# Seven products of a pair in another order: the summed weight block first, three products in one bank

## The chip, the cores and the metric

The kernel runs on one core of one Trainium2 chip. The metric is the device time of one execution in microseconds (us); the figure of a kernel is the median of its runs. Five engines have their own instruction queues: TensorE (PE, with PEld for its weight loads), VectorE (DVE), ScalarE (ACT), GpSimd (POOL) and SyncE (SP). SP, POOL and ACT also start DMA transfers.

## The reference, cut to what matters

One layer of a streaming encoder with 512 frames and a model width of 2048, all in float32:

```
proj = rmsnorm(x) @ w_in          # split into q, k, v, gates, index parts
a = sparse_attention(...) * silu(az)
b = retention(...)        * silu(rz)
merged = sigmoid(ga) * (a @ w_a_out) + sigmoid(gb) * (b @ w_b_out)
r = x + merged @ w_o
y = r + (p @ w_ple) * sigmoid(r @ w_ple_gate)     # then a last rmsnorm
```

The change concerns five of these products: the columns rz, gb, ga and half of az of `w_in`, and `w_o`. Each is a product of a weight of 2048 rows with 512 moving columns.

## The kernel before, in words

**Precision.** A float32 operand is split into a rounded part and the rest (`h`, `l` of a weight, by ACT on line 138 and DVE or POOL on line 144), and the products are summed in PSUM.

**A pair.** The five products above are done two output blocks of 128 at a time, by a scheme of the Strassen-Winograd kind: instead of eight products of quarter size a pair takes seven. The weights of a pair are four blocks of 1024 rows by 128 columns, B11, B12, B21 and B22. The function `block_pair` says how seven stationary operands (units) come out of four raw buffers: buffer `w11` holds B11 and later B11+B12, buffer `t` holds B12+B22, then B11 more, then B21 more, and `w21`, `w22` hold their blocks. Only sums are made on this side. A sum with a block is made by a DMA from HBM that accumulates into the buffer (`add_block`, line 106, issued on POOL's queue: 512 KB each, three for a pair, one of them right after the buffer's first load); the sum of `t` and `w21` is made by DVE (line 146).

**Units ahead.** `gemm_pair` calls `split_to(i + AHEAD)` and `load_to(i + AHEAD + LOADS)` with AHEAD 4 and LOADS 5. So while unit i is multiplied, unit i+3 is split and the raw buffers of unit i+8 are asked for. There are four `wh` and `wl` tiles (W_BUFS), hence the split of a unit waits until the product four units before it is done, and seven raw buffers (RAW_BUFS). The rest of a split (the `wl` subtraction, then the sum into the raw buffer) is queued one step later.

**The moving side.** `combos` makes seven moving operands out of quarters of the input (`PRODUCTS` names them), each 512 wide: 256 columns rounded and 256 columns of rest. For the 22 pairs of `w_in` the input is the normalized x; its operands are made long before, kept in HBM and loaded again during the last retention head (tiles `ha`, `hs`, line 832). For the 8 pairs of `w_o` the input is `merged`; its operands (`ma`, `ms`) are made in four steps for each k, and the last of eight k is made while the first product of the first pair runs.

**A product** is eight k, each one matmul of 512 columns with `wh` (line 253) and one of 256 columns with `wl` (line 254). I count the seven products of a pair as product 0 to product 6. They go into four PSUM banks p, v, q, r in the order p, v, q, r, p, v, r. Behind each product stands what `after` lists: ACT copies (`e1` of p after product 0, `pv` of v after 1, `e2` of p after 4, line 223), DVE combinations (`e_t`, line 227, after products 2, 4, 5 and 6, and `e_d`, line 232, after product 3: r minus pv, which frees r for product 6). `done` adds the two halves of a combination into the output: one DVE addition for the gate pairs (line 854), two for `w_o` (lines 1074 and 1075).

**Order of work.** The order on each queue is the order in which the program writes its instructions; no planner moves them. Every k of a product calls `step`, which runs small pieces of other stages from the lists `todo`, `soon` and `bg`.

Of the kernel before, what the change touches and what calls it, by code (L numbers as in the profile page):

```python
# [9 lines left out]
F32 = mybir.dt.float32  # L10
# [3 lines left out]
AF = mybir.ActivationFunctionType  # L14
OP = mybir.AluOpType
# [19 lines left out]
def block_kernel(tc, xT, pT, posb, posq, w_in, w_v, w_ik, w_a, w_b, w_o, w_ple, w_gate,  # L35
                 w_gt, w_pt, fgb, tab, gains, cst, dec, out, out_a, out_b):
    nc = tc.nc
    pe, dve, act, pool, sp = nc.tensor, nc.vector, nc.scalar, nc.gpsimd, nc.sync

    with contextlib.ExitStack() as ctx:  # L40
# [10 lines left out]
        def U(name, dt=F32):  # L51
            return up.tile([128, L], dt, name=name, tag="u")

        def B(name, dt=F32):
            return bp.tile([128, 1280], dt, name=name, tag="b")

        def P(name):
            return pp.tile([128, L], F32, name=name, tag="p")
# [17 lines left out]
        def raw(src, k0, nk, cols, plus=None):  # L76
            raws.append((src, k0, nk, cols, plus))
            return len(raws) - 1
# [9 lines left out]
        def block_pair(s1, s2):  # L88

            b11, b12, b21, b22 = (s1, 0), (s2, 0), (s1, 8), (s2, 8)
            first = len(units)
            w11 = raw(*b11, 8, 128)
            t = raw(*b12, 8, 128, b22)
            w21, w22 = raw(*b21, 8, 128), raw(*b22, 8, 128)
            for r, plus in ((w11, b12), (t, b11), (w21, None), (w11, None), (t, w21), (t, None), (w22, None)):
                units.append((r, plus, 8, 128))
            return list(range(first, first + 7))

# [22 lines left out]
        def split_to(n):  # L123
            while state["split"] < min(n, len(units)):
                i = state["split"]
                load_to(i + 1)
                r, plus, nk, cols = units[i]
                if r in unfinished:
                    unfinished[r]()
                raw = view(raw_tiles[r], nk, cols)  # L130
                if i in in_raws:
                    t = wp.tile([128, 2, 512], F32R, name="whl", tag="wraw", bufs=RAW_BUFS)
                    h, l = t[:, 0:1], t[:, 1:2]
                elif nk * cols == L:
                    h, l = (U(n, F32R).rearrange("p (a c) -> p a c", c=cols) for n in ("wh4", "wl4"))
                else:
                    h, l = (view(wp.tile([128, 8, 128], F32R, name=n, tag=n), nk, cols) for n in ("wh", "wl"))
                act.activation(h, raw, AF.Copy)  # L138
                e = pool if nk * cols == 1024 and any(a <= i < b for a, b in pool_units) else dve

                def rest(r=r, plus=plus, e=e, l=l, raw=raw, h=h):
                    if unfinished.pop(r, None) is None:
                        return
                    e.tensor_sub(l, raw, h.bitcast(F32))  # L144
                    if isinstance(plus, int):
                        dve.tensor_add(raw, raw, view(raw_tiles[plus], nk, cols))
                    elif plus is not None:
                        add_block(r, plus)

                unfinished[r] = rest  # L150
                later(1 if e is dve else 2, rest)
                loaded[i] = (h, l)
                state["split"] += 1
# [7 lines left out]
        def later(n, f):  # L161
            if n <= 0:
                return f()
            tick[1] += 1
            heapq.heappush(soon, (tick[0] + n, tick[1], f))

        def step():
            tick[0] += 1
            while soon and soon[0][0] <= tick[0]:
                heapq.heappop(soon)[2]()  # L170
            f = todo.popleft() if todo else None
            if f is not None:
                f()
            elif bg and tick[0] % state["rate"] == 0:
                bg.popleft()()
# [34 lines left out]


        LO, HI = slice(0, 256), slice(256, 512)
        PRODUCTS = ("a11", "s3", "a12", "s1", "s2", "a22", "s4")

        def gemm_pair(ids, X, done):


            p, v, q, r = (P("ps_" + n) for n in ("p", "v", "q", "r"))
            E = {}

            def copy(n, src):
                E[n] = U(n)
                act.activation(E[n], src, AF.Copy)

            def out(f, x, y, i, c):
                t = U("e_t")
                f(t, x, y)
                done(t[:, LO], t[:, HI], i, c)

            def fourth():  # L230
                E["d"] = U("e_d")
                dve.tensor_sub(E["d"], r, E["pv"])  # L232

            def fifth():
                copy("e2", p)
                out(dve.tensor_sub, E["d"], E["e2"], 1, HI)

            after = {
                0: lambda: copy("e1", p),
                1: lambda: copy("pv", v),  # L240
                2: lambda: out(dve.tensor_add, q, E["e1"], 0, LO),
                3: fourth,
                4: fifth,
                5: lambda: out(dve.tensor_add, v, E["e2"], 0, HI),
                6: lambda: out(dve.tensor_sub, r, E["e2"], 1, LO),
            }
            for n, (i, o) in enumerate(zip(ids, (p, v, q, r, p, v, r))):
                split_to(i + AHEAD)
                load_to(i + AHEAD + LOADS)
                h, l = loaded[i]  # L250
                for k in range(8):
                    x = X[PRODUCTS[n]][k]
                    pe.matmul(o, h[:, k], x, start=(n < 4 and k == 0), stop=False, skip_group_check=True)  # L253
                    pe.matmul(o[:, LO], l[:, k], x[:, LO], start=False, stop=(k == 7), skip_group_check=True)  # L254
                    step()
                if n in after:
                    after[n]()

        def combos(lo, hi, name, keep=None):


            X = {n: [None] * 8 for n in PRODUCTS}
            T = {}

            def parts(n, k, src):
                t = U(name + n, F32R)
                act.activation(t[:, LO], src, AF.Copy)
                dve.tensor_sub(t[:, HI], src, t[:, LO].bitcast(F32))
                if keep is None:
                    X[n][k] = t  # L270
                else:
                    later(2, lambda: sp.dma_start(keep(n, k), t.bitcast(F32)))

            def sums(k):
                x, y = lo(k), hi(k)
                t1, t2 = T[k] = U("t1"), U("t2")
                dve.tensor_sub(t2[:, LO], x[:, LO], x[:, HI])
                dve.tensor_sub(t1[:, LO], x[:, HI], y[:, HI])
                dve.tensor_sub(t1[:, HI], t1[:, LO], x[:, LO])
                dve.tensor_add(t2[:, HI], y[:, LO], t1[:, HI])  # L280

            def one(k, i):
                if i == 0:
                    parts("a11", k, lo(k)[:, LO])
                    parts("a12", k, hi(k)[:, LO])
                elif i == 1:
                    sums(k)
                    parts("s3", k, T[k][1][:, LO])
                elif i == 2:
                    parts("s1", k, T[k][0][:, LO])  # L290
                    parts("s2", k, T[k][0][:, HI])
                else:
                    parts("s4", k, T.pop(k)[1][:, HI])
                    parts("a22", k, hi(k)[:, HI])

            return X, one
# [10 lines left out]
        for h in range(NH):  # L307
# [4 lines left out]
            else:  # L312
                ids = [block(col(g, h)[:, k:k + 8, :], (8,)) for k in (0, 8) for g in (RQ, RK)]
# [28 lines left out]
        for k in range(KT):  # L342
            if k in (1, 2, 4, 8, 12):
                load_to(state["raw"] + 1)
            if k < 10:
                t = U("xk")
                sp.dma_start(t, xT[:, k, :])
                xs.append(t)
            elif k % 2 == 0:
                t = B("xk2")  # L350
# [287 lines left out]
        hd = dp.tile([56, 128, L], F32, name="hd")  # L638
        x_at = {(n, k): hd[8 * i + k] for i, n in enumerate(PRODUCTS) for k in range(8)}
        xn = {}  # L640
# [183 lines left out]

        Xh = {n: [None] * 8 for n in PRODUCTS}
        x_wanted = collections.deque((n, k) for n in PRODUCTS for k in range(8))

# [36 lines left out]
        for n, u in enumerate(u_rz):  # L864
            y = B("y2")
# [177 lines left out]
        for m in PAIRED:  # L1043
            t = B("sm")
            s, o = t[:, 0:512], t[:, 512:1024]
# [17 lines left out]
        for m in range(8):  # L1063
# [9 lines left out]
            def done(c0, c1, i, q, xc=xc):  # L1073
                dve.tensor_add(xc[i][:, q], xc[i][:, q], c0)
                dve.tensor_add(xc[i][:, q], xc[i][:, q], c1)

            if m == 7:
                todo.extend([None] * 24)
                for k in range(2):
                    t = U("pk")  # L1080
# [9 lines left out]
        for m in range(MF):  # L1090
            i = u_p[m // 4][0]
# [5 lines left out]
            for k in range(2):  # L1097
                a, b = pparts[k]
# [5 lines left out]
            t = U("pw")  # L1104
# [84 lines left out]
        for j in range(4):  # L1189
            pw = P("ps_pw")  # L1190
            wide(u_t[1], pparts, [pw], [j], False)
            y = ys[MF + j]
# [3 lines left out]
        for j in range(4):  # L1196
            dve.tensor_add(acc[0][:, A], acc[0][:, A], sg[j][:, A])
            y = ys[MF + j]
# [48 lines left out]
        for q in range(MF // 4):  # L1247
            o = U("yo")
# [119 lines left out]
```

## Time and profile before

| | |
|---|---|
| median of 3 runs | 1810.67 us (1810.29 to 1814.06) |
| the profiled execution | 1809.38 us |
| its span | 1807.6 us |
| PE busy in the span | 97% |
| DVE, ACT, POOL busy | 67%, 41%, 22% |
| the 22 pairs of `w_in` | 404 to 874 us of the span |
| the 8 pairs of `w_o` | 1434 to 1598 us of the span |

The span runs from the first to the last instruction of the core; the execution is 1.8 us longer. In the views, a row of a timeline has the start, the duration, the engine, the line, the operation, the tiles written and read, the form and, in brackets, the idle time of the engine before it and what ended it. Tiles of a kind share a name, so `wraw` is any raw buffer and `wl` any rest of a weight.

### The profile page before, as it was taken

The page shows a single profiled execution, that of the slowest core. Times are in us where ns is not written, and L with a number is a line of the kernel's source. Part 1 is how long each engine was busy: PE and PEld are TensorE (multiplying, and loading weights), DVE is VectorE, ACT ScalarE, POOL GpSimd, SP SyncE. Part 2 cuts the span into 40 slices and gives each one's busy share as a digit, 9 for nine tenths or more (in the row PEclk, how much of TensorE's full clock was granted, in tenths as well). Part 3 has the DMA queues.
Part 4 walks back from the last instruction along what each step waited for, and adds up shares of the span by engine and source line. Part 5 has one row for each costly group of instructions (what it writes and reads, how often), then busy time and mean ns, then how long its engine had stood idle before and what let it go on. Part 6 is the DMA issues. An engine that isn't in the chain of part 4 may idle for free. (4 is left out here: it accounts for less than half of the span.)

```text
span 1807.6 us, 23881 instructions
## 1 busy us (share of the span) xinstructions
PE 1752.1 (97%) x8966; PEld 1462.5 (81%) x8966; DVE 1210.6 (67%) x1959; ACT 738.1 (41%) x1087; POOL 395.4 (22%) x262
## 2 busy tenths in 40 slices
PE   9999999998999999999999999998989999999997
PEld 7988788887888888888777777886778888878887
DVE  8787874867776667776765357547557878774453
ACT  7464332224444545444532333333334443463332
POOL 2002344432321111110000144354310011111222
PEclk9999999999999999999999999999999999999999
DMA  7327652389878877778875423333236578753312
GB/s 280 110 101 265 227 189 98 102 286 290 231 196 208 209 201 206 201 198 202 295 251 178 135 96 104 106 108 117 71 107 206 161 212 205 174 175 105 94 59 93
DMA packets 114580, 309.65 MB, mean 171 GB/s; under 512 B 12832, under 2 KB 21024, under 8 KB 114464
## 3 DMA queue, kind: packets, MB, share of 16 engines
q1 hardware_dynamic: 91072, 244.15, 40.1%
q0 software_dynamic: 13600, 49.29, 14.7%
q10 hardware_dynamic: 9792, 14.68, 2.4%
q8 instruction: 70, 1.15, 0.3%
q14 instruction: 46, 0.38, 0.1%
HBM read 266.14 MB, written 41.94 MB: 170 GB/s over the span
## 5 line engine op out<-in xcount | busy, mean ns | idle before, releaser
L138 ACT ACTIVATE wh<-wraw 128x1024 fp32r<-128x1024 f32 (+2 forms) x404 | 415.5, 1043 | 535.3 <-issue 100.0
L144 DVE TENSOR_TENSOR wl<-wraw,wh 128x1024 fp32r<-128x1024 f32 (+2 forms) x324 | 401.7, 1243 | 258.7 <-ACT wh L138 258.3
L144 POOL TENSOR_TENSOR wl<-wraw,wh 128x1024 fp32r<-128x1024 f32 x80 | 192.6, 2410 | 339.8 <-ACT wh L138 243.2
L106 POOL DMA_DIRECT2D wraw<-w_in x66 | 58.9, 955 | 366.9 <-DVE wl L144 255.3
L253 PE MATMUL ps_r<-hs,wh 128*128 128x512 f32 x352 | 127.9, 402 | 3.7 <-DVE e_d L232 3.4
L694 PE MATMUL ps_vn<-wh,hh 128*128 128x512 f32 x256 | 102.1, 399 | 0.0
L695 PE MATMUL ps_vn<-wl,hh 128*128 128x512 f32 x256 | 100.1, 391 | 0.0
L696 PE MATMUL ps_vn<-wh,hl 128*128 128x512 f32 x256 | 99.8, 390 | 0.0
L254 PE MATMUL ps_r<-hs,wl 128*128 128x256 f32 x352 | 99.0, 281 | 0.2 <-DVE wl L144 0.2
L253 PEld LDWEIGHTS ps_r<-hs,wh 128*128 128x128 f32 x352 | 66.0, 188 | 23.9 <-issue 8.2
L198 PE MATMUL ps_pg<-rh,wh 128*128 128x512 f32 x192 | 74.7, 389 | 0.0
L199 PE MATMUL ps_pg<-rl,wh 128*128 128x512 f32 x192 | 74.7, 389 | 0.0
L200 PE MATMUL ps_pg<-rh,wl 128*128 128x512 f32 x192 | 74.7, 389 | 0.0
L254 PEld LDWEIGHTS ps_r<-hs,wl 128*128 128x128 f32 x352 | 66.5, 189 | 1.1 <-DVE wl L144 1.0
L106 POOL DMA_DIRECT2D wraw<-w_o x24 | 21.1, 933 | 206.8 <-DVE wl L144 179.2
L709 DVE STREAM_TRANSPOSE bm<-pn 32x320 f32<-32x320 f32 x128 | 64.3, 503 | 1.9
L253 PE MATMUL ps_v<-hs,wh 128*128 128x512 f32 x176 | 65.0, 407 | 0.0
L253 PE MATMUL ps_v<-ha,wh 128*128 128x512 f32 x176 | 63.7, 397 | 0.0
L253 PE MATMUL ps_q<-ha,wh 128*128 128x512 f32 x176 | 63.3, 399 | 0.0
L253 PE MATMUL ps_p<-hs,wh 128*128 128x512 f32 x176 | 63.3, 398 | 0.0
L253 PE MATMUL ps_p<-ha,wh 128*128 128x512 f32 x176 | 63.3, 399 | 0.0
L917 POOL TENSOR_TENSOR bm<-bm,mneg 128x1280 f32<-128x1280 f32 x8 | 21.7, 2708 | 182.1 <-DMA bm<-scr 182.1
(389 smaller groups left out, 4709.3 us busy)
## 6 DMA issues: line engine op xcount, KB each, us to landing
wraw<-w_in SPq DMA_DIRECT2D x174, 512.0 KB, 4.4
wraw<-w_in POOLq DMA_DIRECT2D x66, 512.0 KB, 7.9
wraw<-w_v SPq DMA_DIRECT2D x32, 512.0 KB, 3.9
wraw<-w_o SPq DMA_DIRECT2D x32, 512.0 KB, 4.3
wraw<-w_o POOLq DMA_DIRECT2D x24, 512.0 KB, 7.7
wraw<-w_gate SPq DMA_DIRECT2D x24, 512.0 KB, 4.3
hd<-hs SPq DMA_DIRECT2D x32, 256.0 KB, 2.4
hs<-hd SPq DMA_DIRECT2D x32, 256.0 KB, 5.9
```

What stands on the lines that cost most here:

```text
L106: pool.dma_start(out=raw_tiles[r], in_=src[:, k0:k0 + 8, :], accum_op=OP.add)
L138: act.activation(h, raw, AF.Copy)
L144: e.tensor_sub(l, raw, h.bitcast(F32))
L198: pe.matmul(o, h[:, k, w], a, start=(s == order[0]), stop=False)
L199: pe.matmul(o, h[:, k, w], b, start=False, stop=False)
L200: pe.matmul(o, l[:, k, w], a, start=False, stop=(s == order[-1]))
L253: pe.matmul(o, h[:, k], x, start=(n < 4 and k == 0), stop=False, skip_group_check=True)
L254: pe.matmul(o[:, LO], l[:, k], x[:, LO], start=False, stop=(k == 7), skip_group_check=True)
L694: pe.matmul(pss[t], a[:, tok(t)], h[:, k], start=(s == 0), stop=False)
L695: pe.matmul(pss[t], a[:, tok(t)], l[:, k], start=False, stop=False)
L696: pe.matmul(pss[t], b[:, tok(t)], h[:, k], start=False, stop=(s == KT - 1))
L709: dve.transpose(out=d[32 * a:32 * a + 32, :, 32 * b:32 * b + 32], in_=f[32 * b:32 * b + 32, :, 32 * a:32 * a + 32])
```

## The change

The change does the following:

- In `block_pair` the buffer `t` is the first raw of a pair and not the second, and the units come in the order t, w11, w21, w22, t, t, w11 instead of w11, t, w21, w11, t, t, w22. In words: the first unit is B12+B22, the second B11, the third B21, the fourth B22; then the two larger sums of `t`, and B11+B12 last.
- `PRODUCTS` names the moving operands in the matching order. `s1` and `s2` have the other inner sign, and `a11` is made with its sign turned: ACT multiplies by -1 while it rounds, and DVE takes `scalar_tensor_tensor` in place of a subtraction.
- The banks are v, p, q, r, p, v, p: products 1, 4 and 6 accumulate in p, 0 and 5 in v, one each in q and r.
- After the products: copy `pv` of v after 0, `e1` of p after 1, a combination of q after 2, copy `e2` of p after 4, a combination of v after 5. After 6 come a third copy of p (`e3`), a combination of p with `pv` and one of r with `e3`. There is no `e_d`.

```diff
-            w11 = raw(*b11, 8, 128)
             t = raw(*b12, 8, 128, b22)
-            w21, w22 = raw(*b21, 8, 128), raw(*b22, 8, 128)
-            for r, plus in ((w11, b12), (t, b11), (w21, None), (w11, None), (t, w21), (t, None), (w22, None)):
+            w11, w21, w22 = (raw(*b, 8, 128) for b in (b11, b21, b22))
+            for r, plus in ((t, b11), (w11, b12), (w21, None), (w22, None), (t, w21), (t, None), (w11, None)):
...
-        PRODUCTS = ("a11", "s3", "a12", "s1", "s2", "a22", "s4")
+        PRODUCTS = ("s3", "a11", "a12", "s4", "s2", "a22", "s1")
...
-            def fourth():
-                E["d"] = U("e_d")
-                dve.tensor_sub(E["d"], r, E["pv"])
-
-            def fifth():
-                copy("e2", p)
-                out(dve.tensor_sub, E["d"], E["e2"], 1, HI)
+            def last():
+                copy("e3", p)
+                out(dve.tensor_sub, p, E["pv"], 1, HI)
+                out(dve.tensor_add, r, E["e3"], 1, LO)
...
-                0: lambda: copy("e1", p),
-                1: lambda: copy("pv", v),
-                2: lambda: out(dve.tensor_add, q, E["e1"], 0, LO),
-                3: fourth,
-                4: fifth,
-                5: lambda: out(dve.tensor_add, v, E["e2"], 0, HI),
-                6: lambda: out(dve.tensor_sub, r, E["e2"], 1, LO),
+                0: lambda: copy("pv", v),
+                1: lambda: copy("e1", p),
+                2: lambda: out(dve.tensor_sub, q, E["e1"], 0, LO),
+                4: lambda: copy("e2", p),
+                5: lambda: out(dve.tensor_sub, v, E["e2"], 0, HI),
+                6: last,
...
-            for n, (i, o) in enumerate(zip(ids, (p, v, q, r, p, v, r))):
+            for n, (i, o) in enumerate(zip(ids, (v, p, q, r, p, v, p))):
...
-                dve.tensor_sub(t1[:, HI], t1[:, LO], x[:, LO])
-                dve.tensor_add(t2[:, HI], y[:, LO], t1[:, HI])
+                dve.tensor_sub(t1[:, HI], x[:, LO], t1[:, LO])
+                dve.tensor_sub(t2[:, HI], y[:, LO], t1[:, HI])
...
-                    parts("a11", k, lo(k)[:, LO])
+                    parts("a11", k, lo(k)[:, LO], -1.0)
```

More of the change, by code (lines that the diff above doesn't have):

```diff
@@ L263, in combos, with parts @@
             T = {}
-            def parts(n, k, src):
+            def parts(n, k, src, sign=1.0):
                 t = U(name + n, F32R)
-                act.activation(t[:, LO], src, AF.Copy)
-                dve.tensor_sub(t[:, HI], src, t[:, LO].bitcast(F32))
+                act.activation(t[:, LO], src, AF.Copy, scale=sign)
+                if sign > 0:
+                    dve.tensor_sub(t[:, HI], src, t[:, LO].bitcast(F32))
+                else:
+                    dve.scalar_tensor_tensor(t[:, HI], src, sign, t[:, LO].bitcast(F32), op0=OP.mult, op1=OP.subtract)
                 if keep is None:
```

## The prediction

> **What bounds the kernel now.** I read the page first, then who waited for whom on PE, then the two stages of pairs in stretches, then one pair instruction by instruction.
>
> ```profile
> PE 1752.1 (97%) x8966; PEld 1462.5 (81%) x8966; DVE 1210.6 (67%) x1959; ACT 738.1 (41%) x1087; POOL 395.4 (22%) x262
> ```
>
> PE is the bound, and the change removes no matmul: a pair keeps 7 products of 16 matmuls of the same forms. So time can only come from, or go into, stretches where PE waits.
>
> ```profile
> PE ps_r L253 <- DVE e_d L232: 6.1, 14, 1.7
> PE ps_v L254 <- DVE wl L144: 6.1, 14, 0.6
> PE ps_t L762 <- DVE yn L808: 5.2, 1, 5.2
> PE ps_b L1242 <- POOL rl L1238: 3.7, 1, 3.7
> PE ps_ms L394 <- DVE sq L449: 2.9, 1, 2.9
> PE ps_rs L752 <- DVE ra L722: 2.5, 1, 2.5
> ```
>
> (Columns: who, for whom, us in total, times, longest.) Two of these waits belong to the pairs: a product into v waits for the rest of its weight, and the last product into r waits for `e_d`. Idle time understates their price, since a matmul that starts late is drawn longer. The stretches give the full price (columns: stretch, length, busy time and count of PE, PEld, DVE, ACT, POOL, clock, DMA share, GB/s).
>
> ```profile
> 436.52:874.02 437.50, 427.30 (x2463) 360.98 (x2461) 308.52 (x397) 211.71 (x267) 70.88 (x76) 1.00 0.81 212
> 540.08:560.35 20.27, 20.27 (x126) 17.34 (x125) 14.58 (x20) 10.10 (x13) 2.62 (x3) 1.00 0.85 213
> 727.13:748.30 21.17, 20.41 (x114) 17.13 (x113) 13.87 (x18) 10.08 (x13) 2.67 (x3) 1.00 0.75 199
> 1433.67:1597.94 164.27, 160.04 (x897) 136.98 (x896) 128.34 (x176) 72.32 (x89) 17.53 (x20) 1.00 0.74 194
> 1433.67:1454.22 20.55, 20.03 (x113) 17.15 (x112) 18.34 (x30) 11.25 (x17) 1.88 (x3) 1.00 0.47 145
> 1474.01:1494.02 20.01, 19.98 (x115) 17.15 (x113) 14.74 (x21) 8.60 (x10) 2.64 (x3) 1.00 0.78 204
> 1534.47:1554.26 19.79, 19.79 (x114) 17.15 (x113) 16.24 (x22) 8.67 (x10) 2.62 (x3) 1.00 0.77 183
> ```
>
> The last row is a pair without a wait: 19.79 us for 7 products, 2.83 each. The second is such a pair with 12 small matmuls of another stage between: 20.27, so those cost 0.48. The first row is 21 pairs (all of `w_in` but the first); 2463 matmuls less 21 x 112 leave 9 groups of 12. Without waits it would be 21 x 19.79 + 9 x 0.48 = 419.9, so 17.6 us are lost there. The 8 pairs of `w_o` (fourth row) lose 164.27 - 158.32 = 5.95, of which their first pair (fifth row) 0.76. Pairs with the loss look like the third row. Why it comes about:
>
> ```profile
> 737.43 1.23 DVE L144 TENSOR_TENSOR wl<-wraw,wh 128x1024 fp32r<-128x1024 f32 x1 [2.95 <-ACT wh L138]
> 738.69 1.22 DVE L146 TENSOR_TENSOR wraw<-wraw 128x1024 f32<-128x1024 f32 x1
> 741.04 1.23 DVE L144 TENSOR_TENSOR wl<-wraw,wh 128x1024 fp32r<-128x1024 f32 x1 [1.13 <-ACT wh L138]
> ...
> 744.58 0.69 DVE L232 TENSOR_TENSOR e_d<-ps_r,pv 128x512 f32<-128x512 f32 x1
> 745.18 1.22 DVE L144 TENSOR_TENSOR wl<-wraw,wh 128x1024 fp32r<-128x1024 f32 x1
> 746.31 0.69 DVE L227 TENSOR_TENSOR e_t<-e_d,e 128x512 f32<-128x512 f32 x1
> 747.03 0.42 DVE L854 TENSOR_TENSOR go<-e_t 128x256 f32<-128x256 f32 x1
> 747.37 1.22 DVE L144 TENSOR_TENSOR wl<-wraw,wh 128x1024 fp32r<-128x1024 f32 x1
> ```
>
> ```profile
> 746.80 0.88 POOL L106 DMA_DIRECT2D wraw<-w_in  x1 [17.66 <-DVE wl L144]
> 749.00 1.77 POOL L106 DMA_DIRECT2D wraw<-w_in  x2 [1.32 <-DVE mk L621]
> ```
>
> ```profile
> 736.34 1.06 ACT L138 ACTIVATE wh<-wraw 128x1024 fp32r<-128x1024 f32 x1 [1.58 <-DMA wraw<-w_in]
> ...
> 757.38 1.06 ACT L138 ACTIVATE wh<-wraw 128x1024 fp32r<-128x1024 f32 x1 [0.52 <-DMA wraw<-w_in]
> ```
>
> This is a loop from one pair into the next. At 736.34 the sum B11 has landed in `t`, and ACT splits it for product 4; DVE makes its rest (737.43) and adds `w21` (738.69); ACT splits `t` again, DVE makes that rest (741.04), which product 5 awaits. DVE then works off what has queued: `e_d` (744.58), the rest of the next `w11` (745.18), the combination of product 4, and only then the rest of the next `t` (747.37), behind which POOL sends the next sum into `t` (749.00, the first of the two; the batch's first transfer, at 746.80, is the sum into `w11`). It lands after 8.4 us, and ACT splits it at 757.38. From 736.34 to 757.38 are 21.04 us, more than the 19.79 that PE needs: the loop sets the pace, and PE waits about 1.3 us a pair.
>
> **The change, part by part.**
>
> *The order of the units.* `t` becomes unit 0, so its sum is sent one product earlier while its second use stays product 4. In the loop the rest of the next `t` takes the place of that of `w11`, and `e_d` and the combination of product 4 are gone from between: it would start at 744.58 instead of 747.37, 2.79 us earlier. That makes the loop 18.25 us, below 19.79, and the pace passes to PE. Walked from PE's side, counting from a pair's start: product 3 ends at 11.3 and frees the weight tile, ACT and DVE split the next `t` by 11.3 + 1.06 + 1.23 = 13.6, the sum lands by 13.6 + 8.4 = 22.0, which is 2.2 in the next pair; ACT can split it for product 4 from 2.83. Rests and addition (1.06 + 1.23 + 1.22 + 1.06 + 1.23) end at 8.6; product 5 starts at 5 x 2.83 = 14.2. That is 5.6 us of room where there was none, so the 17.6 us and 5.95 - 0.76 = 5.2 us are there to be won, 22.8 in all. The two ends are 0 and 22.8. Pairs of before without the late rest are not all at 19.79; some take 20.0 (sixth row), so I leave 0.1 for each of 29 pairs, 2.9, and take 19.9.
>
> *What is late next.* The third transfer of the batch, the first sum of the `t` after next, is now wanted for product 0 instead of 1.
>
> ```profile
> DMA to landing us min/median/max: 5.5/7.9/11.7
> ```
>
> (Of line 106.) It is issued behind the sum into `w11`: product 4 ends at 14.2, `e2` takes 0.59, split and rest 2.3, two issues 0.9 each, so at about 18 into the pair. It is there, with the longest landing, 11.7, at 9.9 into the next; ACT wants it at 11.3. On POOL's queue it stands behind two sums that are ready by then, and `qd`, `grs` and the products with `go` stand behind the batch as before.
>
> *The copies and DVE.*
>
> ```profile
> L223 ACT ACTIVATE e<-ps_p 128x512 f32<-128x512 f32 x42 | 24.6, 587 | 7.7 <-ACT go L857 5.7 <-ACT bev L632 1.2 <-PE ps_q L254 0.8
> ```
>
> `e_d` goes: 30 x 0.69 = 20.7 us of DVE. `e3` comes: 30 x 0.587 = 17.6 us of ACT. Neither is on PE's path: in the first stretch ACT is busy 212 of 437 us. If ACT had no room, it would be the 17.6. Behind `e3` on ACT are the split for product 3 of the next pair and the gate function; the gate function waits for the two last combinations, 2 x (0.69 + 0.42) = 2.2 us after product 6, and may make the split for product 4 some 1 us later; that comes out of the 5.6. Product 6 now writes p and so waits for `e2`, which ACT makes during product 5: ready 0.6 after product 4, wanted 2.83 after it. Between 0 and 2.2 us of room used, I take no cost.
>
> *SP.* The load of the first `w22` moves ahead of the 8 last tiles `hs` and delays them by at most 2.5 us (an estimate: 0.524 MB at the 212 GB/s of the first stretch).
>
> ```profile
> 424.99 0.39 SPq L832 DMA_DIRECT2D hs<-hd  x1
> ```
>
> ```profile
> 433.70 0.40 PE L253 MATMUL ps_r<-hs,wh 128*128 128x512 f32 x1
> ```
>
> The last was issued at 424.99 and is first wanted at 433.70; nothing is lost. Before `w_o` one raw's load moves ahead of four small loads: between 0 and 0.524 MB at 194 GB/s (the fourth row), 2.7 us, once; I take nothing, since no row of PE waits for those loads. The scaled `a11` costs 16 longer subtractions, hidden. The 5.2 us wait for `yn` stands ahead of all this and stays.
>
> *The first pair of `w_o`.* Its first product now needs `s3` of the last k, which takes sums first.
>
> ```profile
> 1436.81 0.50 PE L253 MATMUL ps_p<-ma,wh 128*128 128x512 f32 x1 [0.52 <-DVE ma L268]
> ```
>
> ```profile
> 1436.34 0.75 DVE L268 TENSOR_TENSOR ma<-sm,ma 128x256 fp32r<-128x256 f32 x2
> ...
> 1438.60 1.42 DVE L268 TENSOR_TENSOR ms<-t,ms 128x256 fp32r<-128x256 f32 x4
> ```
>
> PE waits 0.52 us for the `ma` that starts at 1436.34. The first `ms` is `s3`; it starts at 1438.60, behind the second `ma` and four sums. So that wait grows by 2.26 to 2.8 us, once. Between 0 and 2.26, I take 2.25: the order on DVE is written out.
>
> **Sum.** 19.9 - 2.25 = 17.65 us gained: 1809.38 becomes 1791.7, its span 1790. The median of the runs is 1.29 above the profiled execution, so 1793.0.
>
> **The rivals.**
>
> *The clock.* A wait of 2.8 us can cost more than itself.
>
> ```profile
> 47.00:54.00 7.00, 6.99 (x27) 7.00 (x28) 2.83 (x6) 0.00 (x0) 1.04 (x1) 0.57 0.30 96
> 184.00:190.00 6.00, 6.00 (x35) 5.09 (x33) 3.30 (x5) 2.14 (x4) 2.40 (x1) 1.00 0.72 236
> 412.00:419.00 7.00, 7.00 (x27) 5.88 (x28) 3.65 (x5) 2.12 (x3) 1.99 (x2) 0.55 1.00 299
> ```
>
> After the wait of 5.2 us (ending near 412) the granted clock is 0.55 for 7 us, after that of 2.9 (near 47) it is 0.57, after that of 2.5 (near 183) it stays 1.00. At 2.8 it may fall: (1 - 0.55) x 7 = 3.1 us more, 1796. The Trainium skill (TensorE: Matmul & The Clock Gate, Part 1: The HAM clock gate) says that the clock falls to half after at least one idle window of about 3.4 us; by that rule 2.8 us would not do it and the sum stays 1793. The trace does not agree at 2.9 us, where the clock fell.
>
> *Half of it.* DVE is busy 309 of 437 us and in order; if its backlog and not the landing holds up product 5, only half of the 22.8 comes: 1810.67 - 11.4 + 2.25 = 1801.5. For it: product 5 waits for DVE by name. Against: DVE itself idles 2.95 us for the landing.
>
> *No change.* POOL's batch lands later as the pairs move closer (DMA share 0.81) and the loop stays at 21: 1810.67 + 2.25, or 1811 to 1813.
>
> *Slower.* One mechanism: ACT is in order, so the third transfer's landing holds the split for the next product 0, behind it `e2`, and thereby product 6 in p. It decides from 15.3 into the pair (6 x 2.83 = 17.0 less 1.06 and 0.59), that is from a landing of 17.1 us, against 11.7 at most now. At 18.5 us the 29 pairs lose 29 x 1.4 = 40.6 against the 17.65 won, 1834.
>
> **How the numbers follow.** The forecast 0.62, the clock 0.20, half 0.08, no change 0.05, slower 0.05. A measurement of this kernel tells 0.2%, 3.6 us, from no change. The first three are faster: 0.90; no change is mostly within the 3.6, so same 0.04 and slower 0.06. The range of 8 in 10 reaches from 1786 (22.8 won and the wait for `s3` hidden would be 1787.9; 2 less for pairs below 19.79) to 1802 (half).
>
> **What would show it.** Right: no row of PE waiting for `wl` in a product into v, nor for an `e_d`; pairs of 19.8 to 20.0 us; POOL's first sum into `t` issued near 14 into the pair; one PE wait for `ms` of about 2.8 us at the start of `w_o`. Wrong: PE waits for `e2` at product 6, ACT idle on a DMA in front of it, or a pace still near 21.

## The result, and the profile after

The changed kernel took 1791.01 us (median of 4 runs, 1787.27 to 1791.93), the kernel before, beside it, 1811.26 (1810.29 to 1814.06): a ratio of 0.9874, with a 95% interval from 0.9854 to 0.9895. Faster by 1.3%; 1793.0 was forecast. The profiled execution is the one of 1787.27 us, with a span of 1785.3; before it was 1809.38 and 1807.6.

The engines' busy times, page of the changed kernel:

```profile
PE 1742.2 (98%) x8966; PEld 1463.7 (82%) x8966; DVE 1198.4 (67%) x1929; ACT 762.7 (43%) x1117; POOL 392.6 (22%) x262
```

The matmuls are as many as before (8966). DVE has 30 instructions fewer (`e_d`), ACT 30 more (`e3`). In the list of who waited for whom on PE (who, for whom, us in total, times, longest), one row above 1 us is new:

```profile
PE ps_v L249 <- DVE ms L265: 2.8, 1, 2.8
```

The two rows of before that belonged to the pairs, 6.1 us each, are gone: no product of a pair waits for a `wl` or an `e_d`. The new wait is that of the first product of `w_o` for `ms`. The stretches, in the same columns as in the prediction:

```profile
436.87:856.80 419.93, 419.93 (x2462) 361.86 (x2461) 301.86 (x378) 229.52 (x290) 68.55 (x76) 1.00 0.87 223
676.69:696.48 19.79, 19.79 (x114) 17.15 (x113) 14.13 (x18) 10.63 (x13) 2.64 (x3) 1.00 0.84 213
1414.23:1575.56 161.33, 158.55 (x898) 137.33 (x896) 126.61 (x169) 78.76 (x96) 17.76 (x20) 1.00 0.79 202
1414.23:1437.05 22.82, 20.04 (x114) 17.16 (x113) 17.65 (x27) 11.58 (x17) 2.63 (x3) 1.00 0.53 143
856.80:1414.23 557.43, 539.75 (x2566) 430.69 (x2565) 342.99 (x619) 200.30 (x336) 135.77 (x60) 0.98 0.45 146
```

The 21 pairs of `w_in` take 419.93 us where they took 437.50: 17.57 less, and PE is busy all of it. The second row is one pair, 19.79. The 8 pairs of `w_o` take 161.33, 2.94 less; all but the first (fourth row, 22.82) are at 19.79. Together that is 20.5 us. The span fell by 22.3; the rest comes from the last row, the attention stage between, which took 559.65 before, 2.2 more, and which the change doesn't touch. In another execution of the changed kernel it took 559.35 (its row stands below, with the clock), so that part belongs to the execution and not to the change.

How the sum into `t` runs now, in one pair (it starts at 676.69, the next one at 696.48). POOL and ACT, each in order of time, and then the landing of POOL's first transfer alone:

```profile
690.96 0.86 POOL L105 DMA_DIRECT2D wraw<-w_in  x1 [15.25 <-DVE mk L620]
694.23 1.78 POOL L105 DMA_DIRECT2D wraw<-w_in  x2 [2.41 <-DVE wl L143]
```

```profile
701.09 1.05 ACT L137 ACTIVATE wh<-wraw 128x1024 fp32r<-128x1024 f32 x1
...
707.86 1.06 ACT L137 ACTIVATE wh<-wraw 128x1024 fp32r<-128x1024 f32 x1 [1.16 <-PE ps_r L249]
```

```profile
DMA to landing us min/median/max: 7.7/7.7/7.7
```

The sum into `t` is sent at 690.96, 14.3 us into the pair, and lands 7.7 later, 2.2 into the next one. The split that needs it is the row at 701.09; it waits for no transfer (no releaser is named), only for its turn on ACT, 2.4 us behind the landing. Before, the corresponding row ended a wait for the DMA. The split for the next pair's product 0 (707.86) waits for PE to free the weight tile, not for its transfer. The rest that product 5 needs is ready on DVE at 707.0, and product 5 starts at 710.6. So the pace is now PE's.

### The profile page after: what moved, and what is told of

Its sections match the earlier page's. It is cut to its first block, busy times and chain, and to the rows that moved or that the text cites. A ratio compares the mean times of both kernels' runs of the same rounds, so it can differ in the third digit from the quotient of the medians.

```text
span 1785.3 us, 23792 instructions
## 1 busy us (share of the span) xinstructions
PE 1742.2 (98%) x8966; PEld 1463.7 (82%) x8966; DVE 1198.4 (67%) x1929; ACT 762.7 (43%) x1117; POOL 392.6 (22%) x262
## 5 line engine op out<-in xcount | busy, mean ns | idle before, releaser
L249 PE MATMUL ps_p<-hs,wh 128*128 128x512 f32 x352 | 126.6, 399 | 0.0
L250 PE MATMUL ps_p<-hs,wl 128*128 128x256 f32 x352 | 98.8, 281 | 0.0
L223 ACT ACTIVATE e<-ps_p 128x512 f32<-128x512 f32 x90 | 53.8, 597 | 103.7 <-PE ps_p L250 101.4
L249 PEld LDWEIGHTS ps_p<-hs,wh 128*128 128x128 f32 x352 | 66.1, 188 | 16.6
L250 PEld LDWEIGHTS ps_p<-hs,wl 128*128 128x128 f32 x352 | 66.5, 189 | 0.0
L249 PE MATMUL ps_r<-hs,wh 128*128 128x512 f32 x176 | 63.8, 401 | 0.0
```

## The experiments

Each time stands beside that of the kernel before on the same chip. The kernels with dead subtractions and those with sums left out ran once each, the others four to ten times.

### The order alone

Units, products and banks in the new order; the old signs, and the last product in q instead of a third one in p. From the kernel before:

```diff
-            for r, plus in ((w11, b12), (t, b11), (w21, None), (w11, None), (t, w21), (t, None), (w22, None)):
+            for r, plus in ((t, b11), (w11, b12), (w21, None), (w22, None), (t, w21), (t, None), (w11, None)):
...
-        PRODUCTS = ("a11", "s3", "a12", "s1", "s2", "a22", "s4")
+        PRODUCTS = ("s3", "a11", "a12", "s4", "s2", "a22", "s1")
...
-            for n, (i, o) in enumerate(zip(ids, (p, v, q, r, p, v, r))):
+            for n, (i, o) in enumerate(zip(ids, (v, p, q, r, p, v, q))):
```

> The new order of units and products alone, in the kernel before: t is unit 0 and its second use stays product 4, but the signs stay as they were, no product is accumulated as a third one in p (the last product goes to q), so DVE keeps five combinations a pair and ACT three copies. Theory (the loop through t set the pace, and the order shortens it): the rest of the next t no longer stands behind a combination, the loop is below 19.79 us, pairs take 19.79 us as in the changed kernel and the time is 1788 to 1793 us. Rival (the gain came from the signs turned in the moving parts, three products in one bank and one DVE instruction of 0.69 us less per pair): pairs stay near 21 us and the time stays nearer 1811 us, above 1803.

It took 1787.79 us against 1812.31, a ratio of 0.987 (0.9847 to 0.9893): the whole gain. The stretch of the 21 pairs of `w_in`:

```profile
436.52:856.45 419.93, 419.93 (x2461) 361.76 (x2460) 316.35 (x401) 219.68 (x269) 68.68 (x76) 1.00 0.87 223
```

419.93 us, as in the changed kernel, though DVE is busy 14.5 us longer (316.35 against 301.86) and more bytes move per us than in the kernel before (223 GB/s against 212). Signs, third accumulation and the dropped `e_d` bring nothing here; the order does it all.

### t second

The changed kernel with its first two units and products exchanged, so that w11 is first and `t` second as before (their banks and copies change places with them), all else as changed.

```diff
-            for r, plus in ((t, b11), (w11, b12), (w21, None), (w22, None), (t, w21), (t, None), (w11, None)):
+            for r, plus in ((w11, b12), (t, b11), (w21, None), (w22, None), (t, w21), (t, None), (w11, None)):
...
-        PRODUCTS = ("s3", "a11", "a12", "s4", "s2", "a22", "s1")
+        PRODUCTS = ("a11", "s3", "a12", "s4", "s2", "a22", "s1")
```

> The changed kernel with the first two units put back: w11 is unit 0 and t unit 1, as before; everything else (signs, three products in p, no e_d) as changed. Theory (the loop): in the loop of 21.04 us the rest of the next w11 (1.22 us less overlap) stands again ahead of that of t, but e_d (0.60 us) and the combination of product 4 (1.06 us) are gone: 21.04 - 0.60 - 1.06 = 19.4 us, just below 19.79, so nearly all pairs still take 19.79 us, the room is 0.4 us and not 1.5, some pairs may wait a few tenths; 1788 to 1797 us, and the wait of the first w_o pair goes back from 2.8 to about 0.5 us. Rival (that t stands first is what does it, the rest brings nothing): pairs near 21 us again and 1805 to 1813 us.

It took 1805.54 us against 1812.31 (ratio 0.9959, 0.9942 to 0.9977), in the rival's range: the expected loop of 19.4 us was wrong. Its stretches, `w_in`, the 20 of these pairs ahead of the last, and `w_o`, and then one row of PE in the last pair of `w_in`:

```profile
435.75:874.59 438.84, 426.45 (x2463) 363.58 (x2462) 299.25 (x383) 226.59 (x292) 70.23 (x76) 0.99 0.81 215
435.75:848.07 412.32, 403.41 (x2338) 344.25 (x2337) 280.89 (x358) 211.88 (x270) 69.80 (x76) 1.00 0.80 212
1433.39:1592.83 159.44, 158.80 (x897) 137.25 (x896) 122.89 (x165) 76.86 (x96) 17.56 (x20) 1.00 0.76 199
```

```profile
869.30 0.80 PE L250 MATMUL ps_p<-hs,wh 128*128 128x512 f32 x1 [3.48 <-ACT e L224]
```

In `w_o` it loses almost nothing. In `w_in` it takes 438.84 us where the kernel before took 437.50, but not all of that is the loop. Of the 18.9 us above the 419.93 of the changed kernel, 12.8 lie in the 20 pairs ahead of the last (these take 399.55 without a wait, as a row further down shows). The other 6.1 lie in the last pair: there product 6 waits 3.48 us for `e2`, which ACT reaches late behind the splits of `bk`, operands of the next stage whose loads it awaits, and the granted clock behind it is 0.58 for 7 us. This is the sign that the prediction gave for its rival "slower", here for another transfer. One turn of its loop, ACT and then POOL, and the landings of the three transfers of that batch:

```profile
609.54 1.06 ACT L138 ACTIVATE wh<-wraw 128x1024 fp32r<-128x1024 f32 x1 [3.92 <-DMA wraw<-w_in]
...
631.01 1.06 ACT L138 ACTIVATE wh<-wraw 128x1024 fp32r<-128x1024 f32 x1 [4.04 <-DMA wraw<-w_in]
```

```profile
619.40 0.88 POOL L106 DMA_DIRECT2D wraw<-w_in  x1 [18.28 <-DMA wraw<-w_in]
620.54 1.80 POOL L106 DMA_DIRECT2D wraw<-w_in  x2 [0.26 <-DVE mk L621]
```

```profile
DMA to landing us min/median/max: 8.2/10.4/14.1
```

The turn takes 631.01 - 609.54 = 21.5 us. From the split at 609.54 to the issue of the sum into `t` (620.54) it is 11.0 us, where it was 749.00 - 736.34 = 12.7 before: the 1.7 us that `e_d` and the combination of product 4 cost are indeed gone. But the sum into `t` now follows the sum into w11 by 1.1 us instead of 2.2, and takes 10.4 us to land instead of 8.4: in both kernels it lands some 3.3 us behind the batch's first transfer, which took 8.2 us here and 7.4 there. I had taken the landing for a constant.

### t second, its sum sent first

The same kernel; POOL holds the sum into w11 until it has sent that into `t`.

```diff
+                    elif plus is not None and plus[1] == 0 and nk == 8 and raws[r][4] is None:
+                        held.append((r, plus))
                     elif plus is not None:
                         add_block(r, plus)
+                        while held:
+                            add_block(*held.pop())
```

> The kernel of the run with t second, in which POOL sends the sum into t ahead of the sum into w11 (the latter is held until t's rest has been made). In the run with t second, the sum into t was sent 1.13 us behind that into w11 and took 10.4 us from issue to landing where it took 8.4 in the kernel before and 7.7 in the changed kernel. Theory (a transfer's landing depends on what was sent just ahead of it, so the order of the units counts twice: the place of the rest, and the place in POOL's batch): sent first, the sum into t lands in 7 to 8.4 us, the loop falls from 21.4 to 18.5 to 19.5 us, and the time from 1805.5 to 1788 to 1794 us. Rival (the longer landing comes from the DMA queues' load as a whole): it stays near 10 us and the time at 1800 to 1808 us.

It took 1786.58 us against 1806.25 (0.9884, 0.9867 to 0.9902). The stretch of `w_in`, a batch on POOL, and the landings of that batch and of its first transfer alone:

```profile
436.81:856.78 419.97, 419.97 (x2463) 361.96 (x2461) 300.49 (x378) 229.47 (x290) 70.41 (x76) 1.00 0.84 224
```

```profile
673.92 2.68 POOL L107 DMA_DIRECT2D wraw<-w_in  x3 [17.09 <-DMA wraw<-w_in]
```

```profile
DMA to landing us min/median/max: 6.2/9.3/12.7
DMA to landing us min/median/max: 6.2/6.2/6.2
```

Three transfers sent within 1.2 us land after 6.2, 9.3 and 12.7 us, one behind the other. The first now is the sum into `t`, and every pair is back at its full pace, though the DMA engines are busier than in the run before (a share of 0.84 against 0.81). So the place in POOL's batch was what held up the run with `t` second; the wait of its last pair is gone too. In the changed kernel the order counts twice: the rest of `t` comes earlier on DVE, and its sum goes out alone, 3.3 us ahead of the other two (690.96 and 694.23).

### More work on DVE, in the loop

The changed kernel with three or six more subtractions after product 3 of every pair, whose result nothing reads, "dead" below (the edit for six).

```diff
+            def dead():
+                E["d"] = U("e_d")
+                for _ in range(6):
+                    dve.tensor_sub(E["d"], r, E["pv"])
...
+                3: dead,
```

> The changed kernel with three more DVE subtractions (128x512, a product's bank less the copy of v) after product 3 of every pair, whose result nothing reads; nothing is left out. They stand in the loop, between the rest of t's second form and the next t's rest. Theory (a loop with slack): about 3 x 0.62 = 1.9 us is added to a loop of 18.25 us or less; the loop comes to 20.1 us at the most, so between nothing and 0.3 us a pair, 0 to 9 us in all: 1787 to 1797 us. Rival (DVE's backlog as throughput bounds the pairs): DVE goes from about 14.5 to 16.4 of 19.79 us, which would cost nothing either; so this run alone shows how much slack the loop has, together with the run of six.

> The changed kernel with six such DVE subtractions after product 3 of every pair. Theory (a loop of latency from pair to pair, 18.25 us or less in the changed kernel): 6 x 0.62 = 3.7 us puts it at up to 21.9 us, so up to 2.1 us a pair once the 5.6 us of room are used up; PE waits for wl in product 5 come back, with some 0.7 to 2.1 us in each of 29 pairs less the room: 1800 to 1840 us. Rival (only DVE's busy time counts): DVE is then busy some 18.2 of 19.79 us, still below, and the time stays within 1787 to 1794 us.

With three it took 1791.28 us, as the changed kernel does; with six 1836.89, slower than the kernel before (1812.31). The 20 pairs of `w_in` between its first and its last, with three and with six:

```profile
439.49:839.04 399.55, 399.55 (x2338) 344.56 (x2337) 323.78 (x420) 216.21 (x271) 68.85 (x76) 1.00 0.83 219
```

```profile
443.12:869.80 426.68, 407.55 (x2339) 347.84 (x2337) 359.89 (x472) 211.36 (x270) 67.06 (x74) 0.99 0.77 204
```

One place in the run with six, on DVE, on PE, on POOL with the landing of that transfer, and on ACT:

```profile
692.38 4.31 DVE L238 TENSOR_TENSOR e_d<-ps_r,pv 128x512 f32<-128x512 f32 x6
696.61 2.35 DVE L143 TENSOR_TENSOR wl<-wraw,wh 128x1024 fp32r<-128x1024 f32 x2
```

```profile
697.88 0.39 PE L256 MATMUL ps_v<-hs,wl 128*128 128x256 f32 x1 [1.17 <-DVE wl L143]
```

```profile
698.23 0.87 POOL L105 DMA_DIRECT2D wraw<-w_in  x1 [18.52 <-DVE wl L143]
DMA to landing us min/median/max: 7.1/7.1/7.1
```

```profile
684.15 1.05 ACT L137 ACTIVATE wh<-wraw 128x1024 fp32r<-128x1024 f32 x1
...
700.06 0.63 ACT L862 ACTIVATE go<-go 128x512 f32<-128x512 f32 x1 [5.23 <-DVE go L859]
...
705.50 1.05 ACT L137 ACTIVATE wh<-wraw 128x1024 fp32r<-128x1024 f32 x1
```

Three, half of 4.31 us a pair, lose nothing: PE is busy all of the 399.55 us. Six lose 426.68 - 399.55 = 27.1, or 1.4 each. So the slack for work at this place is between 2.2 and some 3 us (4.31 - 1.4), where the prediction's loop of 18.25 left 19.79 - 18.25 = 1.5. DVE is busy 359.89 us, 90% of the 399.55 that PE needs, so it isn't DVE's busy time that bounds this run but the place of that work: the rest of the next `t` stands behind it (696.61), and product 0, which started at 696.32, waits for it. That the wait is now in product 0 and not in product 5, as was expected, is new: with `t` first, its rest is wanted at once.

The prediction's loop has come to 21.2 us here: from the split of `t` at 684.15 to the landing at 705.3 (698.23 + 7.1). But the next split starts at 705.50, 0.2 later, and names no transfer. ACT was held by the gate function at 700.06, which had waited 5.23 us for the combination of product 5 on DVE, behind the dead subtractions. This second way round, from DVE to ACT and back, has no landing in it and is a little longer (705.50 - 684.15 = 21.35). So the run shows that a few us in DVE's queue bring a loss back; which of the two ways would do it alone it doesn't show.

### Sums left out

The kernel before, without the transfer that adds B11 into `t`; then also without the one that adds B12 into w11 (the edit of the second).

```diff
-            for r, plus in ((w11, b12), (t, b11), (w21, None), (w11, None), (t, w21), (t, None), (w22, None)):
+            for r, plus in ((w11, None), (t, None), (w21, None), (w11, None), (t, w21), (t, None), (w22, None)):
```

> The kernel before, without the accumulating transfer of B11 into t: t stays B12 + B22 when it is first split, so product 1 and product 4 of each pair use a wrong weight (left out: one sum of 0.5 MB per pair). All engine instructions stay. Theory (the landing of that sum, 8.4 us, is a link of the loop): without it t can be split as soon as its tile is filled and rests wait for products alone; the waits of product 5 for wl go and the time falls to 1786 to 1797 us. Rival (DVE's queue with e_d and the combination of product 4 is the limit by itself): the waits stay and the time stays above 1803 us.

> The kernel before, without the accumulating transfers into w11 and into t (left out: two sums of 0.5 MB per pair; w11 and t keep what they held, so products 1, 3 and 4 use wrong weights). Without the sum into t alone it took 1799.3 us, with waits at product 5 and the sum into w11 landing every 20.4 us. Theory (a second loop, through w11's sum: its landing for product 3's weights holds ACT, in order, and behind it the splits of t): without both sums no pair waits, pairs take 19.79 us, 1786 to 1792 us. Rival (what is left is DVE's queue with e_d and the combination of product 4): the waits at product 5 stay and the time is 1796 to 1801 us.

Without the first, it took 1799.34 us (before: 1812.59), between what the theory and what the rival said: part of the loss is gone, not all. Without both, 1786.06 (before: 1806.25), as the theory of two loops said. The stretches of `w_in`, the one and the other, and then two rows of ACT, one pair apart, in the run that keeps the sum into w11:

```profile
438.38:866.62 428.24, 424.13 (x2463) 361.45 (x2461) 309.93 (x396) 210.05 (x266) 52.92 (x56) 1.00 0.73 191
```

```profile
436.64:856.61 419.97, 419.97 (x2462) 361.93 (x2461) 316.37 (x402) 223.83 (x270) 33.87 (x36) 1.00 0.59 172
```

```profile
686.57 1.06 ACT L138 ACTIVATE wh<-wraw 128x1024 fp32r<-128x1024 f32 x1 [4.70 <-DMA wraw<-w_in]
...
707.04 1.06 ACT L138 ACTIVATE wh<-wraw 128x1024 fp32r<-128x1024 f32 x1 [4.03 <-DMA wraw<-w_in]
```

Of the 17.6 us that `w_in` lost, 9.3 are gone without the one sum (428.24 against 437.50), and all without both. ACT waits for the sum into w11, which is product 3's weight there; ACT works in order, so the splits of `t` stand behind it. From landing to landing are 20.47 us, more than 19.79: a second loop, hidden under the longer one. It too goes through DVE's queue and a landing, and with both landings gone `e_d` and the combination of product 4 make no product wait. (Fewer bytes move as well, 172 GB/s against 212; the run with the order alone, at 223, shows that this isn't what the gain needs.) In the new order w11's second use is product 6, three products later, so this loop goes as well.

### The start of w_o, and the clock

The changed kernel again, and the changed kernel with the sums and `s3` made first for each k:

```diff
                 if i == 0:
-                    parts("a11", k, lo(k)[:, LO], -1.0)
-                    parts("a12", k, hi(k)[:, LO])
-                elif i == 1:
                     sums(k)
                     parts("s3", k, T[k][1][:, LO])
+                elif i == 1:
+                    parts("a11", k, lo(k)[:, LO], -1.0)
+                    parts("a12", k, hi(k)[:, LO])
```

> The changed kernel again, beside the two that follow. Both theories: 1787 to 1793 us. Clock rival: where a run is nearer 1792, the granted clock falls behind the wait of 2.8 us at the start of w_o; where it is nearer 1787, it does not.

> The changed kernel with the order of the steps that make the moving parts turned: the four sums and s3 come first for each k, then a11 and a12. Theory (the wait of 2.8 us at the start of w_o is the place of s3 in DVE's written order): that wait falls to between 0.5 and 1.4 us, and the time by 1.4 to 2.3 us against the changed kernel in the same call, and by up to 3 more where the clock would fall behind the wait. Rival (the wait is for something ahead of both, the end of the stage before): it stays at 2.8 us and the time stays within 0.5 us.

The changed kernel and this one took 1788.43 (1787.42 to 1791.41) and 1789.22 us (1785.38 to 1789.31), beside 1812.59. In the profile the wait falls from 2.8 to 1.4 us as expected; the 1.4 to 2.3 us that were expected of the time can't be told from the scatter. The first matmul of `w_o` and the 7 us behind it, in the changed kernel's first profile, then in its second:

```profile
1419.63 0.50 PE L249 MATMUL ps_v<-ms,wh 128*128 128x512 f32 x1 [2.78 <-DVE ms L265]
```

```profile
1419.00:1426.00 7.00, 6.37 (x36) 5.53 (x37) 4.89 (x9) 4.28 (x8) 0.00 (x0) 1.00 0.18 54
```

```profile
1422.34 0.80 PE L249 MATMUL ps_v<-ms,wh 128*128 128x512 f32 x1 [2.78 <-DVE ms L265]
```

```profile
1422.00:1429.00 7.00, 6.66 (x29) 5.76 (x30) 4.17 (x8) 3.79 (x6) 0.00 (x0) 0.76 0.10 28
1416.93:1441.27 24.34, 21.56 (x114) 18.42 (x113) 17.76 (x27) 11.47 (x17) 2.64 (x3) 0.93 0.49 134
857.58:1416.93 559.35, 541.70 (x2566) 432.23 (x2565) 342.53 (x619) 200.52 (x336) 135.91 (x60) 0.98 0.45 145
```

The same wait of 2.78 us, the same kernel: once the granted clock stays at 1.00, once it is 0.76 over 7 us, and the first pair takes 24.34 instead of 22.82, 1.5 us more. (The last row is the attention stage of the second.)

### yn later

The kernel with s3 first, and the two steps that transpose `yn` of the head before the last moved eight steps later.

```diff
-            todo.extend([None, norm] + [None] * 5 + [scale] + [None] * 5 + [lambda: back(0), None, lambda: back(1)])
+            todo.extend([None, norm] + [None] * 5 + [scale] + [None] * (13 if h == NH - 2 else 5)
+                        + [lambda: back(0), None, lambda: back(1)])
```

> The kernel with s3 first, and the two transposing steps of the head before the last moved eight steps of PE later, so that PE does not come to the transposition before DVE has made yn. Theory (the wait of 5.2 us near 412 and the granted clock of 0.55 for some 7 us behind it are worth their own 5.2 + 3.1 us): the wait goes, and the time falls by 5 to 8 us against the kernel with s3 first. Rival (the loads and splits behind set the end of that stretch, since the same backlog on DVE holds the weights' rests): the wait reappears at the next product, for wl, and the gain is under 2 us.

It took 1792.07 us (1788.93 to 1793.63) against 1812.59: no gain. PE's waits:

```profile
PE ps_kv L774 <- ACT kn L769: 6.5, 1, 6.5
...
PE ps_t L761 <- DVE yn L807: 2.4, 1, 2.4
```

The wait of 5.2 us fell to 2.4, and one of 6.5 for `kn` came in its place. The theory was wrong, and the rival right that the wait comes back elsewhere, though it is for `kn` from ACT and not, as the rival had it, for `wl`.

### Changed kernel and t second with its sum first, side by side

> The changed kernel once more, to stand beside the next one on the same chip: 1784 to 1791 us by both theories. The first product of w_o waits 2.8 us for the last ms, and in most executions the granted clock falls behind it.

> The kernel with t second and its sum sent first, beside the changed kernel on the same chip. Theory (both have pairs of 19.79 us, and this one has a11 first again, so that the wait at the start of w_o is 0.5 us and not 2.8): 2.3 us less than the changed kernel, 1.5 to 2.5 more where the clock falls there: 2 to 5 us faster. Rival (its loop has so little slack that some pairs wait): no faster than the changed kernel, within 1 us or slower.

The changed kernel took 1789.14 us (1785.80 to 1793.48), the other 1787.12 (1786.05 to 1788.33), beside 1806.24: ratios of 0.9904 (0.9885 to 0.9923) and 0.9893 (0.9871 to 0.9914). The 2 us between the medians are what was expected, but the intervals overlap; it isn't shown that one is faster. No version here clearly beats the changed kernel.

## Why the prediction was right

*A loop from pair to pair sets the pace, and the order of the units ends it: right, and shown.* The order alone gives the whole gain, without the landings the gain comes without the order, and 4.31 us more in DVE's queue bring a loss back. The size follows: 17.57 us in `w_in` where the prediction had 17.6 to be won.

*Its reason was incomplete.* The prediction knew one loop and one effect of the order. There were two loops (the second, through w11's sum, at 20.47 us), and the order acts at three places: `t`'s rest earlier on DVE, `t`'s sum first and alone among POOL's transfers, and w11's second use moved from product 3 to 6. By the steps of the prediction `t` second would have done nearly as well (19.4 us); it measured 21.5 us for a turn. The 8.4 us for the landing was treated as a fixed price in the sum, and that it was nearly right (7.7) is luck: the new order happens to send that transfer first. The 5.6 us of room ahead of product 5 were 3.6 (rest ready at 707.0, product at 710.6), mainly because ACT came to the split of `t` 4.6 us into the pair and not at 2.83.

*The term that was mis-sized: "some take 20.0, so I leave 0.1 for each of 29 pairs, 2.9".* The pair of 20.0 us in the prediction (1474.01 to 1494.02) was one that the loop had touched: its last product started only when `e_d` was done.

```profile
1490.33 0.69 DVE L232 TENSOR_TENSOR e_d<-ps_r,pv 128x512 f32<-128x512 f32 x1
```

```profile
1491.16 0.47 PE L253 MATMUL ps_r<-ms,wh 128*128 128x512 f32 x1
```

Without the loop all pairs are at 19.79. Measured are 17.57 + 2.94 = 20.5 us against a sum of 17.65, and 2.9 is the difference. By the sum the profiled execution would have been 1791.7; it was 1787.27, lower by these 2.9 and by the attention stage. That the median came nearer to its forecast (1791.01 against 1793.0) is in part luck: the three other runs were 2.9 to 4.7 us longer than the profiled one. A fall of the clock at the start of `w_o`, see below, can be part of that; those three have no profile.

*The start of `w_o`:* the wait of 2.78 us is the predicted 2.8.

*The clock.* A chance of 0.20 was too little: of six profiles with that wait (the changed kernel three times, the order alone, three and six dead subtractions) the clock fell behind it in five. The price differs. It was 1.5 us in two profiles of the changed kernel. With three dead subtractions the clock was 0.51 over 7 us, and the first pair took 25.29 us where the next one took 19.42, 5.87 more; in the changed kernel without a fall it is 22.82 - 19.79 = 3.03 more, so that fall cost some 2.8, near the 3.1 of the prediction.

```profile
1418.43:1443.72 25.29, 22.51 (x113) 19.31 (x112) 19.64 (x30) 11.47 (x17) 2.63 (x3) 0.87 0.46 125
```

The Trainium skill (TensorE: Matmul & The Clock Gate, Part 1: The HAM clock gate) has the clock fall after an idle window of about 3.4 us; 2.78 us of idling was enough in five of six. The same section of the Trainium skill says that the window runs freely, so that its place differs from run to run. The profiles above agree with that, one wait with two outcomes, but don't show the window itself.

*What was put at nothing was nothing.* ACT is busy 229.5 instead of 211.7 us of the `w_in` stretch and makes nobody wait; no product 6 waits for `e2`; the third transfer is sent some 18 us into the pair (the second of the two at 694.23) and its weights are split when PE frees the tile (707.86, 11.4 into the next), as was worked out. The rivals half, no change and slower did not come. Two things show how near the slower side is. Six dead subtractions a pair were enough: at most some 3 us of slack is all there was. And in the last pair of `w_in`, where ACT also waits for the loads of the next stage, `e2` is ready only 0.15 us before product 6 starts:

```profile
853.28 0.58 ACT L223 ACTIVATE e<-ps_p 128x512 f32<-128x512 f32 x1
```

```profile
854.01 0.41 PE L249 MATMUL ps_p<-hs,wh 128*128 128x512 f32 x1
```

With three dead subtractions product 6 waits 0.48 us there, with six 3.28, and with `t` second 3.48. With the order alone, where that product goes to q, it doesn't wait.

## What to carry to other kernels

When a small wait comes back in every round of a loop, follow it round until it meets itself, and write down its length: instructions in an in-order queue, an issue, a landing. Shorten it by order before work; here the same instructions in another order were worth the 1.3%, and 30 instructions less were worth nothing measurable. A landing has no fixed price: ask what was sent just ahead of it on the same queue, and look for a second loop just below the first. Look at the last round by itself: there the next stage's transfers come in between.

## What was unexpected of the hardware

*Landings queue up.* Three accumulating transfers of 512 KB sent within 1.2 us landed after 6.2, 9.3 and 12.7 us; the sum into `t` was the first in one run and the second, behind the sum into w11, in another, and that alone moved the kernel's time by 0.7% (ratios of 0.9959 and 0.9884). The Trainium skill (DMA: Bandwidth & Descriptors, Issuing engines are not separate DMA queues) says that all transfers share the same 16 engines and interleave; within one batch these landed in turn.

*The same matmuls at two paces, at a granted clock of 1.00.* A pair of `w_o` without a wait, in the run with the order alone:

```profile
1458.12:1477.53 19.41, 19.41 (x114) 17.11 (x113) 16.01 (x22) 8.97 (x10) 2.68 (x3) 1.00 0.88 218
```

It takes 19.41 us, in the changed kernel 19.79, for the same 112 matmuls. All pairs of `w_o` behind the first were at 19.41 in the runs with the order alone and with three dead subtractions; in all three profiles of the changed kernel they were at 19.79. Where the pace changed in these profiles there was a wait or matmuls of another stage, but not every wait changed it, and what decides it stays open. Over 29 pairs it would be 11 us, half of what this change brought.
